# SwiGLU pairs in one decoder block on one core: the product b22 is also made in matmuls of 512 columns, in the first product's two banks

## The chip, the cores and the metric

The kernel is one program on one NeuronCore of a Trainium2 chip. The metric is its time on the device in microseconds (us); the median over runs is compared. A core has a matrix engine (TensorE, PE in the profile; PEld is its loading of stationary weights), a vector engine (VectorE, DVE), an activation engine (ScalarE, ACT), GpSimd (POOL) and SyncE (SP), which here issues the loads. They run side by side and wait for each other through semaphores. Matmuls write into banks of PSUM, which hold 128 partitions x 512 float32 each; everything else is in SBUF or in DRAM.

## The reference, cut to what matters

A decoder block: norm, two token mixers (a convolution and an RG-LRU), a gated merge, a residual, and then a SwiGLU channel mixer with the final norm. The change lies in the channel mixer. With 512 tokens, a model width of 1024 and D_FF = 2816 it computes, in float32:

```
h2  = rmsnorm(x2, norm2_g)                     # 512 x 1024
u   = silu(h2 @ ffn_w1) * (h2 @ ffn_w3)        # 512 x 2816
out = rmsnorm(x2 + u @ ffn_w2, norm_f_g)       # 512 x 1024
```

## The kernel before, in words

The SwiGLU input product is made in 11 "pairs" k = 0 to 10, each of two tiles of 128 columns of D_FF. For a pair the weights form a 2 x 2 block (a half of the 1024 channels by one of the two column tiles), and so do the activations (a half of the channels by a half of the 512 tokens). A scheme with seven block products instead of eight is used, on sums of weight blocks and sums of activation blocks: b11, b21, b22, t1, t2, t3 and t4. Every product is made for both matrices (w1 in the low 256 columns of a bank, w3 in the high ones). Float32 precision comes from splitting weights and activations in a high and a low part and making three matmuls, high x high, high x low, low x high. With four chunks of channels a product is 2 x 4 x 3 = 24 matmuls of 256 columns; `f_product` (L1191) makes them.

Product t1 of pairs 1 to 10 is made otherwise already (`f_wide`, L1201 and L1202). The high and the low part of its activations lie side by side in one tile of 512 columns (`s1b`), so high x high and high x low are one matmul of 512 columns; low x high is one of 256. The two matrices then need a bank each, `fe0` and `fe1`, and each bank holds two halves that have to be added. These two banks come from a PSUM pool of only two buffers (`psum2`), so t1 of the next pair can begin only when both banks have been read. ACT copies the low half into a tile `se` in SBUF (L1298), DVE adds the high half to it (L970), for each bank.

The order of products in the code, and on PE, is for each pair: b11 (for four pairs only; for the others it was made earlier, as was b21), t1, b21, t2, t4 of the pair before, b22, t3. Their sums go like this before the change. t2 is added to b11 in bank `fa`. ACT copies this common sum to a second bank `ft` (L1311). b22 is added to `fa`, t3 to `ft`, and t4 to `ft` as well. After b22, DVE adds `se` to `fa` (L970, 512 columns), ACT makes the silu `sl` (L1264) and DVE the product of the two matrices' halves (L1265). After t3, DVE adds `ft` to `se` and the same two steps follow; after t4 they follow directly from `ft`.

Weights come by SP's loads (`raw_fb`, L352), are summed on DVE (L362 and L119, output `raw_fb`), and split: ACT casts the high part (L123), DVE subtracts it to get the low part (L119). The split tiles are `hl_ft` (for a t product) and `hl_fb` (for a b product), with the pair as suffix in the lists of instructions below. The pool of raw tiles has four buffers, the pool of split tiles five, the pool `short` (`se`, `sl`) five. From pair 7 on, sums of the finished tiles for the output product are made in between on ACT and DVE (`os`, `os1p`, `oe`, `ov`, `ou`). The output product (`or`, L1026) follows the pairs.

Each engine runs its instructions in one fixed order. A scheduler sets it when the program is built, from the code's order and an estimate of times; inside a `manual_schedule` block the named engines keep the code's order.

Of the kernel before, what the change touches and what calls it, by code (L numbers as in the profile page):

```python
# [9 lines left out]
F32R = mybir.dt.float32r  # L10
# [76 lines left out]
def tile_block(ctx, tc, a, out):  # L87
# [9 lines left out]
    def tiles(tag, bufs):  # L97
        p_ = pool(tag, bufs)
        return lambda name, dtype=F32: p_.tile([P, T], dtype, tag=tag, name=name)

    longt, shortt, gatet = tiles("long", SLOTS), tiles("short", SHORT), tiles("gate", GATES)
# [5 lines left out]
    def bank(name):  # L107
        return psum.tile([P, T], F32, tag="mm", name=name)

    def bank2(name):  # L110
        return psum2.tile([P, T], F32, tag="cv", name=name)

    vec, act, pe, pool_e = nc.vector, nc.scalar, nc.tensor, nc.gpsimd
# [77 lines left out]
    def weights(key, ahead=AHEAD):  # L191
        i = next(i for i, c in enumerate(chunks) if c[0] == key)
        emit_to(i + 1 + ahead)
        return held.pop(key)
# [206 lines left out]
    F_ORDER = []  # L401
# [239 lines left out]
    HALVES = [slice(0, 256), slice(256, 512)]  # L641
# [42 lines left out]
    ET = mybir.EngineType  # L684
    with tc.manual_schedule(engines={ET.PE, ET.Activation, ET.DVE, ET.SP}):
# [33 lines left out]
        _, ws, ps = early[0]  # L719
# [235 lines left out]
    for j in range(8):  # L955
        ws = w_tiles(f"lo{j}_0", 5) + w_tiles(f"lo{j}_1", 5)
        ps = bank(f"yb{j}")
# [12 lines left out]
    add = lambda o, x, y: vec.tensor_tensor(out=o, in0=x, in1=y, op=ALU.add)  # L970
    LO, HI = HALVES
# [119 lines left out]
    for n, j in enumerate(mixq.order()):  # L1091
        ws = w_tiles(f"co{j}", ND)
        ps = bank(f"ya{j}")
        mm3(ps, ws, un)
        o = sga[j]
# [11 lines left out]
    for c in range(ND):  # L1107
        if c < ND // 2:
            both_ = longt(f"h2{c}", F32R)
# [70 lines left out]
    o7 = Sevenfold(outq)  # L1180
    f_held = {}

    def f_product(ps, k, x_, w_, again=False, ahead=AHEAD, matrices=range(2)):

        if 0 in matrices:
            f_held[w_, k] = weights(f"f{w_}_{k}", ahead)
        h, l = f_held[w_, k]
        for i in matrices:
            for c, (xh, xl) in enumerate(x_):
                for m, (lw, rx_) in enumerate(((h, xh), (h, xl), (l, xh))):  # L1190
                    pe.matmul(  # L1191
                        ps[:, HALVES[i]], lw[:, 4 * i + c, :], rx_, start=not (again or i or c or m),
                        stop=bool(i and c == 3 and m == 2), skip_group_check=True,
                    )

    def f_wide(banks, k, x_, both_, w_):

        h, l = weights(f"f{w_}_{k}")
        for i, ps in enumerate(banks):
            for c, (xh, _) in enumerate(x_):  # L1200
                pe.matmul(ps, h[:, 4 * i + c, :], both_[c], start=c == 0, stop=False, skip_group_check=True)  # L1201
                pe.matmul(ps[:, LO], l[:, 4 * i + c, :], xh, start=False, stop=c == 3, skip_group_check=True)  # L1202

    kept, opened = {}, {}
# [19 lines left out]
    f_in = {n: [] for n in ("a22", "s1", "s2", "s3", "s4")}  # L1224
# [37 lines left out]
    def f_out(c, dst, sign=1.0):  # L1262
        s_ = shortt("sl")
        act.activation(s_[:, LO], c[:, LO], AF.Silu, scale=sign)  # L1264
        vec.scalar_tensor_tensor(out=dst, in0=c[:, HI], scalar=sign, in1=s_[:, LO], op0=ALU.mult, op1=ALU.mult)  # L1265
# [12 lines left out]
        for k in STARTED[1]:  # L1278
            go_on(k)

    s1_both = [longt(f"s1b{c}", F32R) for c in range(4)]
    for both_, parts_ in zip(s1_both, f_in["s1"]):
        for cs, v in zip(HALVES, parts_):
            nc.sync.dma_start(both_[:, cs].bitcast(F32), v.bitcast(F32))

    seven = {}

    def ffn_product(n, k):

        b_ = seven.setdefault(k, {})  # L1290
        x_ = {"b11": "a11", "b21": "a12", "b22": "s4", "t1": "s1", "t2": "s2", "t3": "s3", "t4": "a22"}[n]
        r = {"b11": "a", "b21": "b", "b22": "a", "t1": "e", "t2": "a", "t3": "c", "t4": "c"}[n]
        if n == "t1" and k:
            wide = [bank2(f"fe{i}_{k}") for i in range(2)]
            f_wide(wide, k, f_in[x_], s1_both, n)
            b_["se"] = shortt(f"se_{k}")
            for cs, ps in zip(HALVES, wide):
                act.copy(b_["se"][:, cs], ps[:, LO])  # L1298
                add(b_["se"][:, cs], ps[:, HI], b_["se"][:, cs])
            return  # L1300
        if n in ("b11", "t1"):
            b_[r] = (bank2 if r == "e" else bank)(f"f{r}_{k}")
        if n == "t2" and k in BEGUN:
            b_[r] = bank(f"f{r}_{k}")
            with tc.issue_after(newest["kept"]):
                act.copy(b_[r], kept[k])
        ps = b_[r]
        f_product(ps, k, f_in[x_], n, n not in ("b11", "t1"))
        if n in ("b11", "t2"):
            new = b_["b" if n == "b11" else "c"] = bank(f"f{n}_{k}")  # L1310
            act.copy(new, ps)  # L1311
            if n == "b11":
                o7.uv[k] = [longt(f"ou{k}"), None]
        elif n == "t1":
            b_["se"] = shortt(f"se_{k}")
            act.copy(b_["se"], ps)
        elif n == "b22":
            add(ps, ps, b_["se"])
        elif n == "t3":
            newest["added"] = add(b_["se"], ps, b_["se"]).ins  # L1320
        if n not in ("b11", "t1", "t2"):
            i, cs = {"b21": (0, LO), "b22": (0, HI), "t3": (1, HI), "t4": (1, LO)}[n]
            if o7.uv[k][i] is None:
                o7.uv[k][i] = longt(f"ov{k}")
            f_out(b_["se"] if n == "t3" else ps, o7.uv[k][i][:, cs], -1.0 if n in ("b22", "t3") else 1.0)
        if n == "t4" and k >= SUMS_FROM:
            o7.pair(k - SUMS_FROM)

    opened_last = list(STARTED[1])
    for n, k in F_ORDER:  # L1330
        ffn_product(n, k)
        if opened_last:
            k = opened_last.pop(0)
            f_out(opened[k], o7.uv[k][0][:, LO])

    x2 = [[longt(f"x2b{t}{h}") for h in range(2)] for t in range(NT)]
    gf = pairt("gf", F32)
# [99 lines left out]
```

## Time and profile before

| | |
|---|---|
| runs before, median (lowest to highest) | 792.45 us (792.34 to 792.89) |
| the profiled execution's own time | 792.59 us |
| its span | 790.8 us |
| the SwiGLU pairs in the trace | 499.0 to 681.2 us |
| busy over the span | PE 99%, DVE 88%, ACT 61%, POOL 28% |

The page of the profile gives busy times, groups of instructions and a chain of work that ended last: the last instruction, what released it, what released that, and so on back to the start. A row of a timeline gives the start and the duration of one instruction (or of several alike in a row, x2), its engine, its line, and output<-inputs by the names above; in square brackets is how long the engine was idle before it and what ended that.

### The profile page before, as it was taken

What the parts mean: (1) busy time and instruction counts of PE and PEld (TensorE: products, weight loads), DVE (VectorE), ACT (ScalarE), POOL (GpSimd) and SP (SyncE); (2) the same over time, 40 slices, a digit from 0 to 9 for tenths busy, and PEclk for the clock granted to TensorE, in tenths of its full rate; (3) what the DMA queues carried; (4) which work ended last, traced back from release to release, by engine and by line L of the source; (5) the groups of instructions that cost most, each with busy time, mean ns of one, the idle gap of its engine ahead of it and who ended that gap; (6) DMA issues with size and microseconds to landing.
All of it is one profiled execution on the core that took longest, in us unless ns stands there. A gap on an engine that the chain in (4) does not pass through costs nothing.

```text
span 790.8 us, 12171 instructions
## 1 busy us (share of the span) xinstructions
PE 783.7 (99%) x4332; PEld 685.9 (87%) x4332; DVE 697.8 (88%) x1050; ACT 483.0 (61%) x712; POOL 222.1 (28%) x172
## 2 busy tenths in 40 slices
PE   9999999999999999999999999999999999999997
PEld 8888888888888888888888899999999999888886
DVE  7699899999989988795797889899989899989867
ACT  7655685987768855562335597555545555585544
POOL 1855766797666856130000000000000000000000
PEclk9999999999999999999999999999999999999999
DMA  6945646487564664458857555554534353786552
GB/s 210 263 130 155 194 137 201 122 244 215 169 201 143 211 186 123 130 173 259 282 185 250 176 168 156 158 154 130 144 107 129 107 149 96 229 291 206 181 173 107
DMA packets 190428, 139.24 MB, mean 176 GB/s; under 512 B 14452, under 2 KB 169504, under 8 KB 190368
## 3 DMA queue, kind: packets, MB, share of 16 engines
q1 hardware_dynamic: 190367, 138.47, 58.0%
q8 instruction: 34, 0.56, 0.3%
q14 instruction: 27, 0.21, 0.1%
HBM read 116.94 MB, written 18.64 MB: 171 GB/s over the span
## 4 chain that ended last, share of the span: by engine, by line
PE 97%; DVE 1%; DMA 1%; issue 0%; SPq 0%; ACT 0%; ACTq 0%
PE z L537 36%; PE or L1026 12%; PE fa L1191 9%; PE ft L1191 8%; PE yb L537 7%; PE ya L537 6%; PE fr L1191 5%; PE mxr L1026 5%; PE g L891 3%; PE fe L1201 2%; PE fb L1191 1%; PE fe L1202 1%; DMA raw_in<-in_w_in_dram 1%; PE th L569 0%; PE z L722 0%; PE fe L1191 0%
## 5 line engine op out<-in xcount | busy, mean ns | idle before, releaser
L766 DVE SCALAR_TENSOR_TENSOR cv<-u,par,cv 128x511 f32<-128x511 f32 (+19 forms) x240 | 162.6, 733 | 5.5 <-ACT cv L763 5.3
L119 POOL TENSOR_TENSOR hl_in<-raw_in,hl_in 128x1024 fp32r<-128x1024 f32 x50 | 121.1, 2427 | 73.5 <-ACT hl_in L123 69.8
L119 POOL TENSOR_TENSOR ows<-ows 128x256 f32<-128x256 f32 x66 | 58.5, 888 | 35.9 <-DMA ows<-in_ffn_w_dram 32.9
L123 ACT CAST hl_ft<-raw_fb 128x1024 fp32r<-128x1024 f32 x44 | 46.0, 1050 | 31.8 <-DVE raw_fb L362 13.3
L119 DVE TENSOR_TENSOR hl_ft<-raw_fb,hl_ft 128x1024 fp32r<-128x1024 f32 x44 | 53.6, 1221 | 9.3 <-ACT hl_ft L123 9.3
L123 ACT CAST hl_in<-raw_in 128x1024 fp32r<-128x1024 f32 x50 | 52.0, 1043 | 12.0 <-PE z L537 6.6
L119 DVE TENSOR_TENSOR hl_fb<-raw_fb,hl_fb 128x1024 fp32r<-128x1024 f32 x33 | 40.0, 1222 | 5.6 <-ACT hl_fb L123 5.5
L362 DVE TENSOR_TENSOR raw_fb<-raw_fb,raw_fb 128x1024 f32<-128x1024 f32 x33 | 40.3, 1221 | 1.5 <-DMA raw_fb<-in_ffn_w_dram 1.2
L123 ACT CAST hl_fb<-raw_fb 128x1024 fp32r<-128x1024 f32 x33 | 34.4, 1051 | 11.5 <-issue 5.0
L537 PE MATMUL z<-h10h,hl_in 128*128 128x512 f32 (+1 forms) x106 | 41.0, 387 | 0.2 <-DVE h10l L593 0.2
L537 PE MATMUL z<-h12h,hl_in 128*128 128x512 f32 (+1 forms) x106 | 40.6, 383 | 0.0
L537 PE MATMUL z<-h13h,hl_in 128*128 128x512 f32 (+1 forms) x106 | 40.6, 383 | 0.0
L537 PE MATMUL z<-h17h,hl_in 128*128 128x512 f32 (+1 forms) x106 | 40.6, 383 | 0.0
L537 PE MATMUL z<-h16h,hl_in 128*128 128x512 f32 (+1 forms) x106 | 40.6, 383 | 0.0
L537 PE MATMUL z<-h11h,hl_in 128*128 128x512 f32 (+1 forms) x106 | 40.5, 383 | 0.0
L537 PE MATMUL z<-h14h,hl_in 128*128 128x512 f32 (+1 forms) x106 | 40.5, 383 | 0.0
L537 PE MATMUL z<-h15h,hl_in 128*128 128x512 f32 (+1 forms) x106 | 40.5, 383 | 0.0
L123 ACT CAST hl_ob<-raw_ob 128x1024 fp32r<-128x1024 f32 (+1 forms) x23 | 23.4, 1015 | 18.6 <-PE or L1026 10.9
L1191 PE MATMUL fa<-hs_1h,hl_fb 128*128 128x256 f32 x176 | 33.5, 283 | 0.0
L1191 PE MATMUL ft<-hs_1h,hl_ft 128*128 128x256 f32 x176 | 33.5, 283 | 0.0
L1191 PE MATMUL fa<-hs_0h,hl_ft 128*128 128x256 f32 x176 | 33.4, 283 | 0.0
L119 DVE TENSOR_TENSOR hl_ob<-raw_ob,hl_ob 128x1024 fp32r<-128x1024 f32 (+1 forms) x23 | 27.1, 1177 | 4.5 <-ACT hl_ob L123 4.2
(958 smaller groups left out, 2519.5 us busy)
## 6 DMA issues: line engine op xcount, KB each, us to landing
raw_fb<-in_ffn_w_dram SPq DMA_DIRECT2D x116, 256.0 KB
raw_in<-in_w_in_dram SPq DMA_DIRECT2D x52, 512.0 KB
ows<-in_ffn_w_dram SPq DMA_DIRECT2D x44, 256.0 KB
os<-ows SPq DMA_DIRECT2D x22, 512.0 KB
raw_ob<-in_ffn_w_dram SPq DMA_DIRECT2D x33, 256.0 KB
raw_ot<-os SPq DMA_DIRECT2D x33, 256.0 KB
raw_lo<-in_lru_w_out_dram SPq DMA_DIRECT2D x16, 320.0 KB
mxws<-in_w_mix_out_dram SPq DMA_DIRECT2D x8, 512.0 KB
```

What stands on the lines that cost most here:

```text
L119: return eng.tensor_tensor(out=o, in0=x, in1=y, op=ALU.subtract)
L123: copy(h, full)
L362: vec.tensor_tensor(out=q, in0=q, in1=y, op=ALU.add)
L537: pe.matmul(ps, l, r, start=i == 0, stop=i == n - 1)
L766: vec.scalar_tensor_tensor(out=acc[c][:, s:], in0=u[c][:, : T - s], scalar=dw(c, s), in1=acc[c][:, s:], op0=ALU.mult, op1=ALU.add)
L891: pe.matmul(ps, l, r, start=k == 0, stop=k == len(mms) - 1)
L1026: pe.matmul(banks[i], l_[:, ts], r_, start=start and n == 0, stop=stop and n == 2, skip_group_check=again)
L1191: pe.matmul(ps[:, HALVES[i]], lw[:, 4 * i + c, :], rx_, start=not (again or i or c or m), stop=bool(i and c == 3 and m == 2), skip_group_c ...
L1201: pe.matmul(ps, h[:, 4 * i + c, :], both_[c], start=c == 0, stop=False, skip_group_check=True)
L1202: pe.matmul(ps[:, LO], l[:, 4 * i + c, :], xh, start=False, stop=c == 3, skip_group_check=True)
```

## The change

For pairs 1 to 10, b22 is made by `f_wide` too, from four more side-by-side tiles (`s4b`, filled by eight more transfers of 128 KB, each half of a tile of 512 columns, behind t1 of pair 0). It accumulates on top of t1 in the banks `fe0` and `fe1`. A new tile `sb` in SBUF receives the two halves of each bank by a copy on ACT (L1296) and an addition on DVE, as `se` does. The common sum after t2 goes to a tile `us` in SBUF (`short`) by the copy that went to the bank `ft` before; `sb` gets `us` added on DVE, and the silu and the product of b22 read `sb`. t3 and t4 accumulate on `fa` itself. The loop over the products stands in a block that keeps PE's order as written.

```diff
-    def f_wide(banks, k, x_, both_, w_):
+    def f_wide(banks, k, x_, both_, w_, again=False):
...
-                pe.matmul(ps, h[:, 4 * i + c, :], both_[c], start=c == 0, stop=False, skip_group_check=True)
+                pe.matmul(ps, h[:, 4 * i + c, :], both_[c], start=c == 0 and not again, stop=False, skip_group_check=True)
                 pe.matmul(ps[:, LO], l[:, 4 * i + c, :], xh, start=False, stop=c == 3, skip_group_check=True)
...
+    def one_tile(name, k, wide):
+
+        o = shortt(f"{name}_{k}")
+        for cs, ps in zip(HALVES, wide):
+            act.copy(o[:, cs], ps[:, LO])
+            add(o[:, cs], ps[:, HI], o[:, cs])
+        return o
...
+        if n == "b22" and k:
+            f_wide(b_["e"], k, f_in[x_], s4_both, n, True)
+            sb = one_tile("sb", k, b_["e"])
+            add(sb, b_["us"], sb)
+            f_out(sb, o7.uv[k][0][:, HI], -1.0)
+            return
         if n == "t1" and k:
-            wide = [bank2(f"fe{i}_{k}") for i in range(2)]
+            wide = b_["e"] = [bank2(f"fe{i}_{k}") for i in range(2)]
             f_wide(wide, k, f_in[x_], s1_both, n)
...
+            b_["se"] = one_tile("se", k, wide)
             return
...
-        if n in ("b11", "t2"):
+        if n == "t2" and k:
+            b_["us"] = shortt(f"us_{k}")
+            act.copy(b_["us"], ps)
+            b_["c"] = ps
+        elif n in ("b11", "t2"):
...
-    for n, k in F_ORDER:
-        ffn_product(n, k)
+    with tc.manual_schedule(engines={ET.PE}):
+        for n, k in F_ORDER:
+            ffn_product(n, k)
+            if (n, k) == ("t1", 0):
+                for both_, parts_ in zip(s4_both, f_in["s4"]):
+                    side_by_side(both_, parts_)
```

The order of products on PE stays, but the order on ACT and DVE shifts. ACT at the end of pair 8, from the cast of t2's weights of pair 9 on, before (`hl_X<-raw_X` are casts of weights, `os1p` is a cast for the output product):

```order
L123 CAST hl_ft_9_6504<-raw_fb_9_6463 128x1024
L1264 ACTIVATE sl<-ft_7_6268 128x256
L123 CAST hl_ft_8_6547<-raw_fb_8_6306 128x1024
L123 CAST os1p_6540<-os_6538 128x256
L123 CAST hl_fb_9_6578<-raw_fb_9_6466 128x1024
L1264 ACTIVATE sl<-fa_6373 128x256
```

and after:

```order
L123 CAST hl_ft_9_6497<-raw_fb_9_6456 128x1024
L1264 ACTIVATE sl<-fa_6229 128x256
L123 CAST hl_ft_8_6540<-raw_fb_8_6302 128x1024
L1296 COPY sb_6559<-fe_8_6397 128x256
L1296 COPY sb_6559<-fe_8_6398 128x256
L123 CAST os1p_6533<-os_6531 128x256
L123 CAST hl_fb_9_6568<-raw_fb_9_6459 128x1024
```

The two copies of `sb`, which wait for the end of b22 of pair 8, now stand ahead of the two casts. DVE at the same place, before:

```order
L119 TENSOR_TENSOR hl_ft_8_6547<-raw_fb_8_6306,hl_ft_8_6547 128x1024
L119 TENSOR_TENSOR os1p_6540<-os_6538,os1p_6540 128x256
L119 TENSOR_TENSOR ov_5061<-ov_5061,oe_6543 128x256
L970 TENSOR_TENSOR fa_6373<-fa_6373,se_6425 128x512
L119 TENSOR_TENSOR oe_6543<-ou_4334,ov_5061 128x256
L119 TENSOR_TENSOR hl_fb_9_6578<-raw_fb_9_6466,hl_fb_9_6578 128x1024
L1265 SCALAR_TENSOR_TENSOR ou_6403<-fa_6373,sl 128x256
```

and after:

```order
L119 TENSOR_TENSOR hl_ft_8_6540<-raw_fb_8_6302,hl_ft_8_6540 128x1024
L119 TENSOR_TENSOR os1p_6533<-os_6531,os1p_6533 128x256
L119 TENSOR_TENSOR ov_5075<-ov_5075,oe_6536 128x256
L970 TENSOR_TENSOR sb_6559<-fe_8_6397,sb_6559 128x256
L119 TENSOR_TENSOR oe_6536<-ou_4334,ov_5075 128x256
L970 TENSOR_TENSOR sb_6559<-fe_8_6398,sb_6559 128x256
L119 TENSOR_TENSOR hl_fb_9_6568<-raw_fb_9_6459,hl_fb_9_6568 128x1024
L970 TENSOR_TENSOR sb_6559<-us_6495,sb_6559 128x512
```

The two additions that free the banks stand where the addition of `se` to `fa` stood, and the third comes behind the next split. DVE at the end of pair 9, before:

```order
L119 TENSOR_TENSOR hl_ft_9_6726<-raw_fb_9_6469,hl_ft_9_6726 128x1024
L119 TENSOR_TENSOR oe_6722<-ou_4995,ov_5255 128x256
L970 TENSOR_TENSOR fa_6637<-fa_6637,se_6632 128x512
L119 TENSOR_TENSOR hl_fb_10_6757<-raw_fb_10_6645,hl_fb_10_6757 128x1024
L1265 SCALAR_TENSOR_TENSOR ou_4704<-fa_6637,sl 128x256
```

and after:

```order
L119 TENSOR_TENSOR hl_ft_9_6716<-raw_fb_9_6462,hl_ft_9_6716 128x1024
L119 TENSOR_TENSOR oe_6712<-ou_5009,ov_5266 128x256
L970 TENSOR_TENSOR sb_6735<-fe_9_6601,sb_6735 128x256
L970 TENSOR_TENSOR sb_6735<-fe_9_6602,sb_6735 128x256
L119 TENSOR_TENSOR hl_fb_10_6744<-raw_fb_10_6635,hl_fb_10_6744 128x1024
L970 TENSOR_TENSOR sb_6735<-us_6671,sb_6735 128x512
```

Here too the additions that free the banks have taken the place of the addition on `fa`; everything ahead of them kept its order.

More of the change, by code (lines that the diff above doesn't have):

```diff
@@ L1279, in tile_block, with side_by_side @@
             go_on(k)
-    s1_both = [longt(f"s1b{c}", F32R) for c in range(4)]
-    for both_, parts_ in zip(s1_both, f_in["s1"]):
+    s1_both, s4_both = ([longt(f"{n}b{c}", F32R) for c in range(4)] for n in ("s1", "s4"))
+    def side_by_side(both_, parts_):
         for cs, v in zip(HALVES, parts_):
             nc.sync.dma_start(both_[:, cs].bitcast(F32), v.bitcast(F32))
+    for both_, parts_ in zip(s1_both, f_in["s1"]):
+        side_by_side(both_, parts_)
     seven = {}
+    def one_tile(name, k, wide):
[4 more added lines that the diff above has]
+        return o
     def ffn_product(n, k):
@@ L1292, in ffn_product @@
         r = {"b11": "a", "b21": "b", "b22": "a", "t1": "e", "t2": "a", "t3": "c", "t4": "c"}[n]
+        if n == "b22" and k:
[4 more added lines that the diff above has]
+            return
         if n == "t1" and k:
-            wide = [bank2(f"fe{i}_{k}") for i in range(2)]
+            wide = b_["e"] = [bank2(f"fe{i}_{k}") for i in range(2)]
             f_wide(wide, k, f_in[x_], s1_both, n)
[L1296 to L1299, printed above, removed]
+            b_["se"] = one_tile("se", k, wide)
             return
@@ L1329, in tile_block @@
     opened_last = list(STARTED[1])
-    for n, k in F_ORDER:
-        ffn_product(n, k)
-        if opened_last:
-            k = opened_last.pop(0)
-            f_out(opened[k], o7.uv[k][0][:, LO])
+    with tc.manual_schedule(engines={ET.PE}):
[3 more added lines that the diff above has]
+                for both_, parts_ in zip(s4_both, f_in["s4"]):
+                    side_by_side(both_, parts_)
+            if opened_last:
+                k = opened_last.pop(0)
+                f_out(opened[k], o7.uv[k][0][:, LO])
     x2 = [[longt(f"x2b{t}{h}") for h in range(2)] for t in range(NT)]
```

## Prediction

> **What bounds the kernel now.** I read the page's busy times and its chain first, then busy times over the stretch of the SwiGLU pairs, then the chain in order of time there, and last the timelines of DVE, ACT and SP where DVE runs late.
>
> ```profile
> PE 783.7 (99%) x4332; PEld 685.9 (87%) x4332; DVE 697.8 (88%) x1050; ACT 483.0 (61%) x712; POOL 222.1 (28%) x172
> ...
> PE 97%; DVE 1%; DMA 1%; issue 0%; SPq 0%; ACT 0%; ACTq 0%
> ```
>
> PE is busy for 99% of the span and makes 97% of the chain, so a gain must come from PE's own work, and any wait put on PE costs its full length.
>
> ```profile
> 499.00:681.20 182.20, 182.20 (x1440) 178.04 (x1439) 165.21 (x211) 98.64 (x152) 0.00 (x0) 1.00 0.45 132
> 639.00:681.20 42.20, 42.20 (x333) 41.04 (x333) 40.02 (x59) 23.96 (x39) 0.00 (x0) 1.00 0.44 136
> ```
>
> The columns are the stretch, its length, busy us of PE, weight loads, DVE, ACT and POOL, the granted clock, and the transfers. Over all pairs PE never idles. DVE is idle for 182.20 - 165.21 = 17.0 us, but only for 2.2 us of the last 42: there it is nearly as full as PE.
>
> ```profile
> 565.34 0.23 PE fe L1201
> ...
> 614.14 0.23 PE fe L1201
> ...
> 642.83 2.88 PE fa L1191 x24
> 645.71 2.88 PE ft L1191 x24
> 648.59 0.23 PE fe L1201
> ...
> 651.42 2.87 PE fa L1191 x24
> ...
> 660.06 2.88 PE ft L1191 x24
> 662.94 0.23 PE fe L1201
> ...
> 677.28 0.93 PE or L1026 x4
> 678.22 3.03 PE ft L1191 x24
> 681.24 97.29 PE or L1026 x428
> ```
>
> The chain shows start and length. A narrow product takes 2.88 us (b22 of pair 8 from 642.83, t3 from 645.71). A wide one, t1 of pair 9, takes 651.42 - 648.59 = 2.83. The other rows give where t1 of pairs 4, 7 and 10 start: 565.34, 614.14, 662.94.
>
> **The change part by part.**
>
> *PE.* Ten products go from 2.88 to 2.83 us: 0.05 each, **-0.5** in all. All of it is on the path, if nothing else makes PE wait. It is also the largest gain that these rows allow.
>
> *DVE and ACT, work.* Durations come from the starts of neighbours on DVE, where it runs without a pause:
>
> ```profile
> 645.60 0.42 DVE L119 TENSOR_TENSOR os1p<-os,os1p 128x256 fp32r<-128x256 f32 x1
> 645.93 0.42 DVE L119 TENSOR_TENSOR ov<-ov,oe 128x256 f32<-128x256 f32 x1
> 646.26 0.69 DVE L970 TENSOR_TENSOR fa<-fa,se 128x512 f32<-128x512 f32 x1
> 646.86 0.42 DVE L119 TENSOR_TENSOR oe<-ou,ov 128x256 f32<-128x256 f32 x1
> 647.20 1.22 DVE L119 TENSOR_TENSOR hl_fb<-raw_fb,hl_fb 128x1024 fp32r<-128x1024 f32 x1
> ...
> 651.86 0.76 DVE L970 TENSOR_TENSOR se<-fe,se 128x256 f32<-128x256 f32 x2
> 653.86 1.23 DVE L362 TENSOR_TENSOR raw_fb<-raw_fb,raw_fb 128x1024 f32<-128x1024 f32 x1 [1.24 <-DMA raw_fb<-in_ffn_w_dram]
> ...
> 670.74 0.69 DVE L119 TENSOR_TENSOR ous2l<-ou,ous2h 128x512 fp32r<-128x512 f32 x1
> ...
> 651.46 0.37 ACT L1298 COPY se<-fe 128x256 f32<-128x256 f32 x1 [0.20 <-PE fe L1202]
> ```
>
> 256 columns occupy DVE for 0.33 us (645.60 to 645.93), 512 for 0.60 (646.26 to 646.86), and 512 from SBUF alone take the same 0.69 as from PSUM (670.74 against 646.26). Before, b22 needs one addition of 512. After, it needs two of 256 and one of 512: +0.66 us per pair, 6.6 in ten. It lies beside PE's work as long as DVE's 17.0 us of idle time cover it; in the last 42 us they are 2.2, so there it can show. ACT gets two more copies of 0.37 (the row at 651.46) per pair, 7.4 us into 182.20 - 98.64 = 83.6 of idle time: free as work, not free in order (below). The copy of the common sum stays, of the same size, to another place. That t3 and t4 now accumulate on `fa` adds no wait: t4 of the pair before and b22, 5.7 us, lie between t2's end and t3.
>
> *Eight more transfers on SP.* Their kind is in the trace, for `s1b`:
>
> ```profile
> 493.19 0.51 SPq L1284 DMA_DIRECT2D s1b<-hs_0l  x1
> 493.80 0.55 SPq L1284 DMA_DIRECT2D s1b<-hs_0h  x1
> ...
> 506.67 1.23 DVE L119 TENSOR_TENSOR hl_ft<-raw_fb,hl_ft 128x1024 fp32r<-128x1024 f32 x1 [1.29 <-ACT hl_ft L123]
> ...
> L1201 PE MATMUL fe<-s1b,hl_ft x80: 395/398/403, 513.5 to 665.2; 128*128 128x512 f32 x80
> ```
>
> They are issued 0.61 us apart, so eight hold SP's queue for 4.9 us at most, ahead of loads of weights. The nearest consumer is t1 of pair 1: its weights are split by 506.67 + 1.23 = 507.90 and PE needs them at 513.5. The 5.6 us between cover 4.9; my estimate is some 2 us of delay, from where the transfers stand among the loads. The first b22 made wide is later still. Cost 0; without the cover it would be at most the 4.9.
>
> *The release of the two banks.* This is the new wait. Before, t1 of the next pair finds both banks read long ago. After, they are held until b22's `sb` additions. In DVE's order these stand where the addition on `fa` stands in the rows here, so that row says when they come:
>
> ```profile
> 562.66 0.69 DVE L970 TENSOR_TENSOR fa<-fa,se 128x512 f32<-128x512 f32 x1
> ...
> 611.47 0.69 DVE L970 TENSOR_TENSOR fa<-fa,se 128x512 f32<-128x512 f32 x1
> ...
> 662.21 1.23 DVE L119 TENSOR_TENSOR hl_ft<-raw_fb,hl_ft 128x1024 fp32r<-128x1024 f32 x1
> 663.34 0.42 DVE L119 TENSOR_TENSOR oe<-ou,ov 128x256 f32<-128x256 f32 x1
> 663.68 0.70 DVE L970 TENSOR_TENSOR fa<-fa,se 128x512 f32<-128x512 f32 x1
> ...
> 677.35 0.69 DVE L970 TENSOR_TENSOR se<-ft,se 128x512 f32<-128x512 f32 x1
> ```
>
> For pair 3 the addition starts at 562.66 and t1 of pair 4 at 565.34: a first addition of 0.42 leaves 2.3 us. For pair 6 it is 611.47 against 614.14, also 2.2; for pair 8, 646.26 against 648.59, 1.9. What DVE and ACT do later than before comes off these margins: I expect 1.0 to 1.1 us to be left at pairs 3, 6 and 8, so **0** there. The second bank is used half a product, 1.42 us, later and has more. For pair 9 the addition starts at 663.68, *after* t1 of pair 10 at 662.94. DVE was 3.6 us behind b22's end at 660.06 without anyone waiting; now PE waits.
>
> How much later DVE stands at 663.68 than before is set one pair earlier:
>
> ```profile
> 644.58 0.41 ACT L123 CAST os1p<-os 128x256 fp32r<-128x256 f32 x1 [0.39 <-DVE os L970]
> 645.79 1.05 ACT L123 CAST hl_fb<-raw_fb 128x1024 fp32r<-128x1024 f32 x1 [0.81 <-PE fa L1191]
> ...
> 648.45 1.83 SPq L352 DMA_DIRECT2D raw_fb<-in_ffn_w_dram  x3
> ```
>
> The `os1p` cast at 644.58 now stands behind two copies that wait for b22 of pair 8, which ends at 645.71 less the 0.4 that eight wide b22 have gained: 645.31. The second copy occupies ACT till about 645.7, the cast till 646.03, and DVE's `os1p` starts at 646.06 instead of 645.60. Then come `ov` 646.40, the first `sb` addition 646.73, `oe` 647.06, the second 647.40, and `hl_fb` 647.73 instead of 647.20: 0.53 later. SP's load at 648.45 is issued when that split has ended (647.20 + 1.22 = 648.42), so it lands 0.53 later and DVE, which waited 1.24 us for it, resumes at 654.39 instead of 653.86. Its own work is done at 652.62 (651.86 + 0.76) + 0.53 + 0.60 = 653.75, so this wait takes up all lateness but the 0.53. From there DVE runs without a pause to 663.68, in the same order in both kernels. The first `sb` addition of pair 9 then starts at 663.68 + 0.53 = 664.21 and ends at 664.63; t1 of pair 10 starts some 0.06 later, at 664.69. PE would be ready at 662.94 - 9 x 0.05 = 662.49: a wait of 2.2 us. Against before, t1 starts 664.69 - 662.94 = +1.75 later; b22 of pair 10 still gives back 0.05: **+1.7**.
>
> Bounds for this step: if DVE is not late at all, 663.68 + 0.42 + 0.06 - 662.94 = +1.2. If none of the 0.66 of nine pairs (5.9) is absorbed, 1.2 + 5.9 = +7.1. I take +1.7, near the lower end, because the DVE wait at 653.86 absorbs. As the forecast's own spread I take +1.2 to +2.3 (a second 0.53 from a pair's ACT order).
>
> *Behind it.* t4 of pair 10 writes the bank that DVE's addition at 677.35 has read by 678.04; it starts at 678.22, behind four `or` matmuls. DVE there is 0.53 + 2 x 0.66 = 1.85 later at most, about 1.65 with a pause taken up, and PE is 1.7 later, with one more `or` matmul of 0.93 / 4 = 0.23 ahead: no further wait. The 97.29 us of `or` shift as a whole.
>
> **The sum** on the profiled execution of 792.59 (0.14 above the median): -0.45 + 2.2 - 0.05 = +1.7, 794.3. On the median, 792.45 + 1.7 = **794.2**. A measurement here can tell about 0.2%, 1.6 us, from no change: below 790.9 is faster, above 794.0 slower.
>
> **The rivals.**
>
> *PE does not wait (not slower).* The mechanism is the same bank at pair 9; it decides if the first `sb` addition ends before 662.5, 1.6 us sooner than the row at 663.68 ends its first 0.42. For it: DVE idles 1.24 us at 653.86, so a load landing sooner would move all behind it. Against: that load hangs on the split before, which comes later. Then only -0.5 stays: 791.95. The same time results if the additions are issued sooner than I read.
>
> *More banks come late.* DVE does not recover its 0.66 per pair, and t1 of pairs 4, 5, 7 or 9 waits as well. It decides when DVE is some 1.0 us later than I assume at pairs 3, 6 or 8. For it: the margins of 1.0 are small beside six pairs' 4.0 us of work, and copies at the head of ACT's order delay casts. Against: 17.0 us of idle time. Between the +2.3 and +7.1 I take half of the 5.9 absorbed: 1.2 + 2.95 = 4.15, 796.6.
>
> *The wait lowers PE's clock.* PE hardly ever pauses in this trace; the nearest row is at the start:
>
> ```profile
> 8.00:9.60 1.60, 1.24 (x10) 0.96 (x9) 1.41 (x5) 1.42 (x4) 0.41 (x1) 1.00 1.14 326
> ```
>
> There PE was idle for 0.36 of 1.60 us, and the granted clock stayed 1.00; no row shows a pause of 2.2 us. If one product behind the wait were made at half the pace, it would cost another 2.88: 797.1. The Trainium skill, TensorE: Matmul & The Clock Gate, section "What's actually happening", says that the array's clock is halved after an idle window of about 3.4 us and restored after a busy one of that length; by it a wait of 2.2 us would change nothing if it stays shorter than the window, which speaks for my sum, and a longer one (the second rival) would bring this case about. No run here shows it.
>
> *Matmuls of 512 columns are cheaper in a long stream (faster).* If high x (high, low) cost as much as one narrow matmul, 2.88 / 24 = 0.12, a b22 would fall to 16 x 0.12 = 1.92, and ten give -9.6: 782.9. Against: ten such products already stand in this trace, at 2.83. The same page, section "Back-to-back issue gap", gives about 131 ns for 512 columns in a sustained stream; by that figure, as an estimate, a b22 would take 8 x (0.131 + 0.12) = 2.0 us. The trace disagrees (8 x (x + 0.12) = 2.83 makes x 0.23), and the measurement decides.
>
> **How the numbers follow.** Forecast .52: its spread of +1.2 to +2.3 ends at 793.65 to 794.75, so .24 of it lies within 0.2% and .28 above. No wait .14 (same). More banks late .27 (slower). Clock .03 (slower). Cheaper matmuls .04 (faster). That is faster .04, same .38, slower .58. The range 791.9 to 796.6 leaves out the cheaper matmuls, the clock and nearly half of the second rival (.12): .19. The forecast's own range is 793.6 to 794.8.
>
> **What would show it.** In the profile after: b22 on `fe` at 2.83 us; t1 of pair 10 starting 2 us behind t3's end with DVE's `sb` addition as the releaser; no such wait at t1 of pairs 4, 7 and 9; an ACT `os1p` cast behind the `sb` copies and a `hl_fb` split half a us later at pair 8. If PE waits at other pairs too, or not at pair 10, or the wait is not DVE's, the prediction is wrong.

## The result and the profile after

The changed kernel takes 797.17 us in the median of its first six runs (795.83 to 798.38), against 792.51 before: a ratio of 1.0058 with a 95% interval of 1.0045 to 1.0070. It is slower by 4.7 us, not by 1.7, and its runs lie far apart, where those of before stay within 0.6 us. The profiled execution took 797.93 us with a span of 796.2. Two executions of this case, one of the kernel before (1308.6 us, granted clock 0.556) and one of e7 below (4348.6 us, 0.168), are in the slow state and stay out of the ratios.

Busy times and chain of the changed kernel:

```profile
PE 784.9 (99%) x4252; PEld 683.0 (86%) x4252; DVE 701.8 (88%) x1070; ACT 488.3 (61%) x732; POOL 220.7 (28%) x172
...
PE 91%; DVE 5%; DMA 2%; issue 1%; ACT 1%; SPq 0%; ACTq 0%; DVEq 0%
```

The shares of busy time are those of before. The chain is not: DVE and DMA now hold 7% of it, where PE alone held 97%. The table of waits on PE in the stretch of the pairs (us in total, times, the longest) says for what:

```profile
PE fe L1201 <- DVE sb L970: 4.1, 2, 2.5
```

The busy times by stage (stretch, length, PE, weight loads, DVE, ACT, POOL, granted clock, transfers) say where:

```profile
520.00:540.00 20.00, 17.46 (x118) 16.27 (x118) 18.14 (x27) 10.09 (x19) 0.00 (x0) 0.91 0.59 170
...
660.00:690.00 30.00, 28.46 (x197) 26.42 (x197) 28.45 (x46) 17.81 (x32) 0.00 (x0) 1.00 0.40 130
```

PE waits twice, both times for a bank that a `sb` addition still reads: once between 660 and 690, and once, longer, between 520 and 540. There the granted clock is 0.91 as well. PE's timeline at both places:

```profile
530.58 0.28 PE L1191 MATMUL fa<-hs_1h,hl_ft 128*128 128x256 f32 x1
533.39 0.50 PE L1201 MATMUL fe<-s1b,hl_ft 128*128 128x512 f32 x1 [2.54 <-DVE sb L970]
...
533.85 0.40 PE L1201 MATMUL fe<-s1b,hl_ft 128*128 128x512 f32 x1
...
535.07 0.63 PE L1201 MATMUL fe<-s1b,hl_ft 128*128 128x512 f32 x1
...
537.63 0.41 PE L1191 MATMUL fa<-hs_0h,hl_ft 128*128 128x256 f32 x1
...
668.32 0.47 PE L1201 MATMUL fe<-s1b,hl_ft 128*128 128x512 f32 x1 [1.53 <-DVE sb L970]
```

The first wait, 2.54 us, is at t1 of pair 2. A microsecond behind it the 512-column matmuls go from 0.40 to 0.63 us, and the product takes 537.63 - 533.39 = 4.24 us instead of 2.83. The second wait, 1.53 us, is the forecast one at t1 of pair 10. Waits of 2.54 and 1.53, some 1.5 for the slower clock, less 0.5 of gain: 5.1 of the 5.3 us by which this execution (797.93) lies above that of before (792.59).

Why DVE is late at pair 2 starts 25 us earlier. The kernel before, from the timelines of SP's queue (from 490 to 505) and of DVE, and the start of t1 of pair 2 from its chain:

```profile
496.37 7.40 SPq L352 DMA_DIRECT2D raw_fb<-in_ffn_w_dram  x8
...
504.16 1.23 DVE L362 TENSOR_TENSOR raw_fb<-raw_fb,raw_fb 128x1024 f32<-128x1024 f32 x1
...
528.85 0.69 DVE L970 TENSOR_TENSOR fa<-fa,se 128x512 f32<-128x512 f32 x1
...
530.88 0.23 PE fe L1201
```

And SP's queue, in the same stretch, and DVE in the changed kernel:

```profile
500.97 0.60 SPq L1285 DMA_DIRECT2D s4b<-hs_1l  x1
501.67 3.35 SPq L352 DMA_DIRECT2D raw_fb<-in_ffn_w_dram  x6
...
508.52 1.23 DVE L362 TENSOR_TENSOR raw_fb<-raw_fb,raw_fb 128x1024 f32<-128x1024 f32 x1 [4.33 <-DMA raw_fb<-in_ffn_w_dram]
...
532.93 0.74 DVE L970 TENSOR_TENSOR sb<-fe,sb 128x256 f32<-128x256 f32 x2
```

The loads of pair 1 began at 496.37; behind the eight `s4b` transfers they begin at 501.67, 5.3 us later. DVE's sum for t1 of pair 1 moves from 504.16 (the `raw_fb` sum of before) to 508.52. From there DVE catches up hardly anything until the `sb` additions of pair 1, at 532.93, where the addition on `fa` stood at 528.85. t1 of pair 2 waits for the first of them.

### The profile page after: what moved, and what is told of

It is laid out like the page before. It is cut to its first block, busy times and chain, and to the rows that moved or that the text cites. A ratio compares the mean times of both kernels' runs of the same rounds, so it can differ in the third digit from the quotient of the medians.

```text
span 796.2 us, 12060 instructions
## 1 busy us (share of the span) xinstructions
PE 784.9 (99%) x4252; PEld 683.0 (86%) x4252; DVE 701.8 (88%) x1070; ACT 488.3 (61%) x732; POOL 220.7 (28%) x172
## 4 chain that ended last, share of the span: by engine, by line
PE 91%; DVE 5%; DMA 2%; issue 1%; ACT 1%; SPq 0%; ACTq 0%; DVEq 0%
PE z L537 35%; PE or L1026 12%; PE fa L1191 10%; PE yb L537 7%; PE ya L537 5%; PE fr L1191 5%; PE mxr L1026 5%; PE fe L1201 4%; PE g L891 3%; PE fe L1202 2%; DVE hl_ft L119 1%; PE fb L1191 1%; DVE raw_fb L362 1%; DMA raw_in<-in_w_in_dram 1%; DMA raw_fb<-in_ffn_w_dram 1%
## 5 line engine op out<-in xcount | busy, mean ns | idle before, releaser
L1201 PE MATMUL fe<-s1b,hl_ft 128*128 128x512 f32 x80 | 30.1, 414 | 4.1 <-DVE sb L970 4.1
L1191 PE MATMUL fa<-hs_1h,hl_ft 128*128 128x256 f32 x160 | 30.4, 283 | 0.0
```

The lines of the kernel that those rows point to most:

```text
L1191: pe.matmul(ps[:, HALVES[i]], lw[:, 4 * i + c, :], rx_, start=not (again or i or c or m), stop=bool(i and c == 3 and m == 2), skip_group_c ...
L1201: pe.matmul(ps, h[:, 4 * i + c, :], both_[c], start=c == 0 and not again, stop=False, skip_group_check=True)
```

## The experiments

All changes are against the changed kernel unless said otherwise. The times of before beside them were taken on the same chip.

**The changed kernel again (e1_again).**

> The changed kernel once more, for its spread. Its six runs lie in two groups, 795.8 to 796.4 and 797.9 to 798.4 us. Theory clock: the groups differ by whether TensorE's granted clock falls behind the wait at t1 of pair 2; the runs near 798 have a mean clock of 0.996 to 0.997 and those near 796 of 0.998 to 1.0, and nothing lies between. Rival: the wait itself varies, then the times spread without groups and do not go with the clock.

Six runs: 793.88 to 797.74, median 796.91 against 792.59 (ratio 1.0050, 1.0036 to 1.0063). The times do not form two groups with nothing between: 793.88 lies below them, and 795.69, 796.49 and 797.34 close most of the gap. The clock, though, divides the twelve runs of this kernel as the first theory says: the six from 797.34 us up have a mean granted clock of 0.996 or 0.997, the six up to 796.49 one of 0.998 or more. The profile is of the 793.88 run; from its timelines of DVE and PE:

```profile
505.64 1.23 DVE L362 TENSOR_TENSOR raw_fb<-raw_fb,raw_fb 128x1024 f32<-128x1024 f32 x1 [1.94 <-DMA raw_fb<-in_ffn_w_dram]
...
530.35 0.75 DVE L970 TENSOR_TENSOR sb<-fe,sb 128x256 f32<-128x256 f32 x2
...
530.82 0.50 PE L1201 MATMUL fe<-s1b,hl_ft 128*128 128x512 f32 x1 [0.46 <-DVE sb L970]
...
664.25 0.47 PE L1201 MATMUL fe<-s1b,hl_ft 128*128 128x512 f32 x1 [1.54 <-DVE sb L970]
```

And its busy times at pair 2, in the columns of above:

```profile
520.00:540.00 20.00, 19.54 (x146) 18.55 (x146) 18.49 (x25) 10.18 (x16) 0.00 (x0) 1.00 0.58 167
```

Here the same loads let DVE go on at 505.64, not 508.52; the wait at pair 2 is 0.46 us, the clock stays at 1.00, and the wait at pair 10 is again 1.54. So the lateness behind the transfers itself varies between executions, by 2.9 us in these two. Of these, 1.2 are there already when SP issues the loads (at 500.43 in e1_again, 501.67 in the first profile); why the rest of the time to landing differs is open. Together with the clocks, the times fit a short wait, a long wait, and a long wait with a slower clock; only two of the twelve executions have a profile.

**The transfers behind the loads of pair 1 (e2_late).**

```diff
-            if (n, k) == ("t1", 0):
+            if (n, k) == ("b22", 0):
                 for both_, parts_ in zip(s4_both, f_in["s4"]):
```

> The eight s4b transfers are issued behind the weight loads of pair 1 instead of ahead of them; nothing else changes. Theory transfers (the loads of pair 1 land 4.3 us later, DVE is as late until pair 1's sb additions, so t1 of pair 2 waits 2.5 us): that wait is gone and only the one at t1 of pair 10 is left, as the prediction had it: 794.2 us, and no fall of the clock at pair 2. Rival work (DVE's 0.66 us more per pair makes the lateness): t1 of pair 2 still waits over 1 us, 796 to 798.

792.85 us in eleven runs (792.53 to 792.97) against 792.59: ratio 1.0003 (0.9994 to 1.0012). The wait at pair 2 and the spread are gone, as the theory of the transfers says: moving the eight transfers takes 4.1 us off the 796.91 of e1_again, some of it at pair 10 (below). The other wait is shorter than it had it:

```profile
504.42 1.23 DVE L362 TENSOR_TENSOR raw_fb<-raw_fb,raw_fb 128x1024 f32<-128x1024 f32 x1 [0.20 <-DMA raw_fb<-in_ffn_w_dram]
...
528.91 0.75 DVE L970 TENSOR_TENSOR sb<-fe,sb 128x256 f32<-128x256 f32 x2
...
663.29 0.47 PE L1201 MATMUL fe<-s1b,hl_ft 128*128 128x512 f32 x1 [0.78 <-DVE sb L970]
```

DVE is on time, and t1 of pair 10 waits 0.78 us. One move of a few transfers made the scheduler order ACT differently too: at pair 8 the `os1p` cast now stands between the two `sb` copies and no longer behind both. ACT in e2_late:

```profile
644.02 0.38 ACT L1296 COPY sb<-fe 128x256 f32<-128x256 f32 x1
644.29 0.41 ACT L123 CAST os1p<-os 128x256 fp32r<-128x256 f32 x1
645.39 0.37 ACT L1296 COPY sb<-fe 128x256 f32<-128x256 f32 x1 [0.69 <-PE fe L1202]
```

ACT in e1_again:

```profile
644.21 0.37 ACT L1296 COPY sb<-fe 128x256 f32<-128x256 f32 x1
645.58 0.37 ACT L1296 COPY sb<-fe 128x256 f32<-128x256 f32 x1 [0.99 <-PE fe L1202]
645.85 0.41 ACT L123 CAST os1p<-os 128x256 fp32r<-128x256 f32 x1
```

The cast comes 1.5 us sooner. This is the head of ACT's order that the prediction priced, undone by accident; the 0.76 us between the two waits goes with it, but other orders moved as well, so that is not shown alone.

**Banks of even pairs from the other pool (e3_banks).**

```diff
-            wide = b_["e"] = [bank2(f"fe{i}_{k}") for i in range(2)]
+            wide = b_["e"] = [(bank2 if k % 2 else bank)(f"fe{i}_{k}") for i in range(2)]
```

> The wide banks of even pairs come from the other PSUM pool (six banks), so t1 of the next pair never needs a bank that sb still holds; the transfers stay where the change put them. Theory banks: both waits (pair 2 and pair 10) vanish though DVE is as late as in the changed kernel, 792.0 us (the gain of 0.45 alone). Rival: DVE's lateness makes PE wait for weights instead, 794 or more.

794.36 us (793.76 to 795.49) against 792.59: 1.0023 (1.0015 to 1.0032). Both waits for `sb` are gone with the transfers in place, and in this profile DVE is late at pair 2 (it goes on at 506.34 and reaches the `sb` additions of pair 1 at 532.19). So the held banks are what turns DVE's lateness into PE's there. But not to 792.0: other waits stand in the profile. From the table of waits, and below it from PE's timeline:

```profile
PEld fa L1191 <- ACT fa L1321: 1.0, 2, 0.6
```

```profile
697.50 1.43 PE L1026 MATMUL or<-hl_ob,ous4h 128*128 128x512 f32 x5 [0.30 <-ACT ous4h L123]
```

t2 waits for ACT's copy of the kept sum, and the output product for the sums `ous4` that ACT and DVE make for it. Each theory had half of it.

**Before, with the transfers alone (e4_copies).** The eight transfers are put into the kernel before at the same place; nothing reads them.

> The kernel before with only the eight s4b transfers added at the place that the change gives them; nothing reads them. Theory: loads and DVE are 4 us late around 508 to 530 but no bank is held for DVE, so PE does not wait, 792.5 us (within 0.3). Rival: the transfers cost time by themselves, 794 or more.

792.79 us against 792.59: 1.0004 (0.9995 to 1.0013). DVE is late here too, and PE does not wait:

```profile
506.46 1.23 DVE L362 TENSOR_TENSOR raw_fb<-raw_fb,raw_fb 128x1024 f32<-128x1024 f32 x1 [2.28 <-DMA raw_fb<-in_ffn_w_dram]
...
532.03 0.69 DVE L970 TENSOR_TENSOR fa<-fa,se 128x512 f32<-128x512 f32 x1
```

The addition on `fa` comes 3.2 us later than before (528.85) and costs nothing. (One of the eleven runs, at 794.30, has no profile.) It needs both parts of the change, late loads and held banks, to make the wait.

**PE kept busy in the wait (e5_fill, e12_fill_half).** Twenty matmuls of 256 columns, or five of 512, into a spare bank ahead of t1 of pair 2:

```diff
+            if k == 2:
+                spare = bank("spare")
+                h_, _ = f_held["t3", 1]
+                for i in range(FILL):
+                    pe.matmul(spare[:, LO], h_[:, i % 8, :], f_in["s1"][i % 4][0], start=True, stop=True, skip_group_check=True)
             f_wide(wide, k, f_in[x_], s1_both, n)
```

> The changed kernel with 20 more matmuls of 256 columns into an unread bank of PSUM ahead of t1 of pair 2; their results are not used. They take 20 x 0.12 = 2.4 us, about the longest wait seen there. Theory clock (a wait of 2.5 us lets the clock fall, and the half clock then costs 1.6 us): t1 of pair 2 starts no later than it did after the long wait, the clock stays at 1.00, and every run comes out at -0.5 + 2.4 + 1.5 = +3.4, near 796.0 us, none above 796.6. Rival: the clock falls for another reason, then runs of 797 to 798.4 remain.

(As run, e5 does not compute the block: its twenty matmuls each start an accumulation anew in one half of their bank, and they disturb a sum of the block; which one was not looked into. The other instructions and their sizes are those of the changed kernel. In e12 the five open and close one whole bank, and it does compute the block.) 795.41 us, 794.81 to 795.83 in five runs, against 792.76: 1.0033 (1.0020 to 1.0046). Though 2.4 us of useless matmuls were added, it is 1.5 us faster than the median of e1_again, and no run is above 795.83. Half of that is another thing: the scheduler gave e5 the order of e2 on ACT, and its wait at pair 10 is 0.78 us instead of 1.54.

```profile
530.73 2.56 PE L1318 MATMUL spare<-hs_0h,hl_ft 128*128 128x256 f32 x20
533.18 0.50 PE L1202 MATMUL fe<-s1b,hl_ft 128*128 128x512 f32 x1
```

DVE is as late here as in the changed kernel's first profile (the `sb` additions start at 532.71, there at 532.93), so without the twenty PE would have paused about as long. t1 of pair 2 starts at 533.18, near the 533.39 there, without a pause. The busy times from 533.3 to 537.9 in the changed kernel:

```profile
533.30:537.90 4.60, 4.51 (x18) 3.89 (x19) 4.60 (x8) 0.85 (x2) 0.00 (x0) 0.65 0.73 207
```

And in e5_fill:

```profile
533.30:537.90 4.60, 4.60 (x31) 4.24 (x32) 4.60 (x7) 1.91 (x4) 0.00 (x0) 1.00 0.77 226
```

The granted clock is 0.65 behind the pause and 1.00 without it, so it falls because of the pause. The sum comes out as well: -0.5 + 2.4 + 0.8 = 2.7, measured 2.65.

> As e5, with 5 matmuls of 512 columns into the spare bank (5 x 0.23 = 1.2 us, not used), so that a part of the wait at t1 of pair 2 stays. Theory clock (only the long pause of some 2.5 us lets the clock fall): the pause that is left is at most 1.4 us and the clock stays at 1.00, so the runs lie between -0.5 + 1.2 + 0.8 = +1.5 (794.1 us, DVE little late) and -0.5 + 2.5 + 0.8 = +2.8 (795.4, DVE as late as in the first profile), none above 796. Rival (any pause may lower the clock): some runs of 796.5 to 798.

794.96 us against 792.84 (1.0032, 1.0021 to 1.0042). Seven of eight runs lie between 794.5 and 795.54, as expected; one, at 796.56, does not, and it has no profile, so whether its clock fell or its loads came later still stays open (its mean granted clock is 0.998). In none of the thirteen runs of e5 and e12 is that mean below 0.998, where six of the twelve of the changed kernel had 0.996 or 0.997.

```profile
530.78 1.33 PE L1318 MATMUL spare<-s1b,hl_ft 128*128 128x512 f32 x5
533.18 0.51 PE L1202 MATMUL fe<-s1b,hl_ft 128*128 128x512 f32 x1 [1.07 <-DVE sb L971]
```

In the profiled run a pause of 1.07 us was left, and the clock of this stretch stayed at 1.00.

Two profiles of experiments further down (e9, e10) hold long pauses at another place, t4 of pair 10, from other waits. PE of e9 and the busy times behind it, then the same of e10:

```profile
683.20 0.58 PE L1191 MATMUL fa<-h24h,hl_ft 128*128 128x256 f32 x1 [2.52 <-DVE se L970]
683.20:687.80 4.60, 4.60 (x25) 4.58 (x26) 2.69 (x5) 0.94 (x3) 0.00 (x0) 0.65 0.40 139
```

```profile
683.64 0.39 PE L1191 MATMUL fa<-h24h,hl_ft 128*128 128x256 f32 x1 [2.25 <-DVE se L970]
683.60:688.20 4.60, 4.56 (x25) 4.56 (x26) 2.73 (x5) 0.93 (x2) 0.00 (x0) 0.63 0.39 134
```

The clock falls there as well. So in the profiles of this case all three pauses of 2.25 us and more in the pairs were followed by a lower clock, and none of those up to 1.54 us was.

**The transfers on another queue (e8_queue).** `side_by_side` issues `s4b` by `nc.gpsimd.dma_start`, at the same place in the program.

> The changed kernel with the eight s4b transfers issued by GpSimd's queue, at the same place in the program, so they stand ahead of no weight load. Theory order (SP issues one after the other, the loads of pair 1 wait behind them): DVE is on time at pair 1 and only t1 of pair 10 waits, 1.5 us: 793.6 us. Rival bandwidth (the transfers take the loads' share wherever they are issued): DVE is still over 2 us late at pair 1, 795 or more.

792.90 us against 792.76: 1.0000 (0.9991 to 1.0008). From DVE's timeline, and below it a row of the list of what uses `s4b` (GpSimd's issues, with the first and the last start):

```profile
504.20 1.23 DVE L362 TENSOR_TENSOR raw_fb<-raw_fb,raw_fb 128x1024 f32<-128x1024 f32 x1 [0.17 <-DMA raw_fb<-in_ffn_w_dram]
```

```profile
L1285 POOL DMA_DIRECT2D s4b<-hs_1h x4: 538/538/686, 475.5 to 487.8; - x4
```

DVE is on time, so off SP's queue the transfers cost nothing. But the second row (four of the eight; the others are issued from 476.8 to 491.1) shows that the same bytes did not move at the same time: GpSimd issued them all before SP's loads, which start at 496.19, while SP in the changed kernel issued them from 496.50 to 500.97. So e8 does not decide between the two theories. That the place in SP's queue costs time is seen in the 5.3 us by which the loads are issued later; whether the transfers' share of bandwidth adds to it was not separated. (The wait at pair 10 is 0.8 us here, again with e2's order on ACT.)

**Without the last wait (e6_late9, e7_both).** e6 is e2 with b22 of pair 9 in narrow matmuls on `fa`, the copy of t2's sum to a bank included:

```diff
+NARROW = (0, 9)
...
-        if n == "b22" and k:
+        if n == "b22" and k not in NARROW:
...
-        if n == "t2" and k:
+        if n == "t2" and k not in NARROW:
```

> As e2 (transfers behind the loads of pair 1), and b22 of pair 9 is made as before the change, in narrow matmuls on fa, so no bank waits for DVE ahead of t1 of pair 10. Theory banks: the last wait (0.8 us in e2) is gone and 9 x 0.05 = 0.45 us of gain is left, 792.1 us. Rival: DVE's work in the last pairs costs time anyway, 792.8.

e7 is e2 and e3 together.

> Transfers as in e2 and banks as in e3. Theory banks: no wait for a bank at all, 792.1 us if the small waits of e3 (on ACT's copy of the kept sum, and 0.9 us in the output product) came from DVE's lateness. Rival: they came from the new order on ACT and DVE, then 793 to 794.

Both lie further above before than e2 did (0.26 us), though the intervals overlap: e6 793.48 us against 792.76 (1.0010, 1.0001 to 1.0019), e7 793.36 (1.0008, 0.9999 to 1.0017). No t1 waits for a bank in either. The wait has moved to the output product. Busy times of e6 there, and below them a row of its PE:

```profile
692.00:700.00 8.00, 7.70 (x34) 6.03 (x33) 5.74 (x10) 4.50 (x7) 0.00 (x0) 1.00 1.04 377
700.00:708.00 8.00, 7.57 (x32) 5.61 (x31) 6.99 (x11) 7.68 (x12) 0.00 (x0) 1.00 0.68 237
```

```profile
705.27 1.91 PE L1027 MATMUL or<-hl_ob,ous6h 128*128 128x512 f32 x7 [0.32 <-ACT ous6h L124]
```

Before, each of these stretches holds 37 matmuls; here 34 and 32, eight fewer at 8.00 / 37 = 0.22 us: 1.7 us. Ahead of `or`, PE had won its 0.5; the sums `ous4` and `ous6` were not ready sooner, and more than the gain is lost on them. The times are those of the rivals; which of their causes it is, DVE's work or the new order, these two runs do not separate.

**The third addition on GpSimd (e9_pool, e10_both_pool).** In e2 and in e7:

```diff
-            add(sb, b_["us"], sb)
+            pool_e.tensor_tensor(out=sb, in0=sb, in1=b_["us"], op=ALU.add)
```

> As e2, and the third addition of each pair (sb plus the common sum, both in SBUF) is made by GpSimd, which is idle in this stretch, instead of DVE; DVE then has 0.06 us more per pair than before the change instead of 0.66. Theory DVE (what is left of the gain is eaten by DVE's work in the last pairs, as a wait at t1 of pair 10 or in the output product): DVE stands some 0.6 us earlier at pair 9, the 0.8 us wait shrinks below 0.3 and the output product does not wait, 792.2 us against e2's 792.85 and 792.6 to 792.8 before. Rival: the slower addition on GpSimd delays the silu and the product behind it on DVE, 793 or more.

> As e7 (late transfers, banks from two pools), and the third addition of each pair on GpSimd. Theory DVE: with no bank to wait for and DVE's load as before, neither the pairs nor the output product wait: -0.45, 792.2 us, against e7's 793.36. Rival: the waits in the output product come from the order of the sums for it, not from DVE's load: 793 or more.

799.0 us and 798.85 against 792.64 (1.0076, 1.0063 to 1.0088; 1.0073, 1.0061 to 1.0086). The group on GpSimd in e9, and below it the table of DVE's waits:

```profile
L1308 POOL TENSOR_TENSOR sb<-sb,us 128x512 f32<-128x512 f32 x10 | 19.3, 1932 | 309.5 <-DVE sb L970 309.5
```

```profile
DVE ou L1265 <- ACT sl L1264: 11.1, 9, 1.6
```

One addition takes 1.93 us there instead of 0.69. The silu starts that much later, DVE stands behind it for up to 1.6 us in its fixed order, and with it everything that PE needs: 6.0 us saved as work, 11.1 lost as waits. PE then pauses for DVE and its clock falls (the rows of e9 and e10 above). The test says nothing on DVE's load alone.

**Wide b22 in pairs 1 to 6 only (e11_late6).** As e6, with `NARROW = (0, 7, 8, 9, 10)`.

> As e2, with b22 wide only in pairs 1 to 6; pairs 7 to 10, where DVE also makes sums for the output product, are as before the change. Theory DVE: six pairs have idle time for 0.66 us each, so 6 x 0.05 = 0.3 us is won and nothing waits: 792.3 to 792.5 us. Rival: the lateness of six pairs (4 us of work) is carried into the last ones and the output product waits, 793 or more.

792.21 us (eleven runs, 792.0 to 792.99) against 792.64: 0.9997 (0.9988 to 1.0006). PE is busy throughout from 520 to 760; its rows from 660 on:

```profile
660.00:690.00 30.00, 30.00 (x203) 27.63 (x202) 28.11 (x47) 16.74 (x26) 0.00 (x0) 1.00 0.56 176
690.00:760.00 70.00, 70.00 (x311) 57.95 (x310) 61.01 (x88) 43.86 (x62) 0.00 (x0) 1.00 0.69 223
```

This is the lowest median of all: it is 0.43 us below that of before, where 0.3 was expected, but the interval does not separate it from no change. The six early pairs do absorb their 0.66 us of DVE work.

## Why the prediction was wrong, point by point

**The step that failed: "Eight more transfers on SP", put at a cost of 0.** Its upper bound, 4.9 us of delay in SP's queue, was about right (5.3 in the first profile, 4.1 in e1_again); the "some 2 us" that it took instead was not. And it looked at one consumer, the weights of t1 of pair 1, which were indeed ready in time. It did not follow DVE further: DVE runs almost without a pause from there to 529, so 4.1 us of lateness came out at the `sb` additions of pair 1, and a term put at 0 cost a wait of 2.54 us and, behind it, 1.5 us of slower clock in that execution. The step on the banks listed margins for pairs 3, 6, 8 and 9 and left out pair 1, whose 528.85 (plus 0.42) against t1 of pair 2 at 530.88 left 1.6 us; 4.1 less 1.6 is the wait of 2.5. e2 and e8 (wide b22, transfers out of the loads' way) and e4 (transfers alone) cannot be told from before, and e3 (both, but no bank held) has no wait there: it takes late loads and held banks together.

**The wait at t1 of pair 10: right place, mis-sized.** 2.2 us was forecast, 1.54 measured in both profiles of the changed kernel. The 0.53 us of lateness carried from pair 8 was not there. In e1_again the split `hl_fb` ended 0.8 us later than before, as the order on ACT had it, but the load behind it did not land later:

```profile
653.91 1.22 DVE L362 TENSOR_TENSOR raw_fb<-raw_fb,raw_fb 128x1024 f32<-128x1024 f32 x1
...
663.68 0.75 DVE L970 TENSOR_TENSOR sb<-fe,sb 128x256 f32<-128x256 f32 x2
```

DVE went on at 653.91 without a wait for the transfer, and the first `sb` addition stands at 663.68, exactly where the addition on `fa` stood. So the lower bound, +1.2 for a DVE that is not late, was the value to take; the execution with hardly any wait at pair 2 came out there, 793.88 against 792.59. Two readings behind the 0.53 do not hold. From 653.86 on DVE does pause, for 0.51 us at 656.20 in before (for a cast on ACT that follows DVE's own sum, so it absorbs nothing), and its order is not quite the same: the product `ov` that stood at 661.21 is made at 657.46 in e1_again. And the 0.06 us from the addition's end to t1, which no row showed, were 0.15 (663.68 + 0.42 to 664.25).

**The clock: a rival given .03, and true in several runs.** Its price of one product at half pace, 2.88 us, was too high: from the start of t1 of pair 2 to the end of t4 of pair 1 the changed kernel takes 537.84 + 5.91 - 533.39 = 10.36 us by the first row below (from its chain), and e1_again 533.91 + 5.76 - 530.82 = 8.85 by the second (from the chain of that execution): 1.5 us. The slower stretch begins only 1.2 us after PE resumes and lasts some 3.5 us. Its place was wrong as well: pair 2, not pair 10. That the rival's 797.1 lies beside the measured 797.17 is chance, since it adds too high a price to a sum that lacks the wait at pair 2.

```profile
537.84 5.91 PE fa L1191 x48
```

```profile
533.91 5.76 PE fa L1191 x48
```

The Trainium skill, TensorE: Matmul & The Clock Gate, section "What's actually happening", puts the idle window at about 3.4 us; here pauses of 2.54, 2.52 and 2.25 us were enough, while pauses of 0.78 to 1.54 left the clock at 1.00. The measurement decides.

**What held.** b22 on `fe` takes 2.83 us. No t1 of pairs 4, 5, 7 and 9 waits in any profile of the changed kernel, so the margins of 1.0 us and DVE's idle time sufficed, and "more banks come late" did not happen as written, though one more bank did come late, by another cause and at a pair that it does not name. t4 of pair 10 does not wait. With the transfers out of the way (e8, e2) what is left is the forecast mechanism, a smaller wait at pair 10 (0.78 us, with another order on ACT than the one that was forecast from), at +0.1 to +0.3 us.

**What the -0.5 is worth.** The sum took it as won on PE. e6 and e7 show that, with no bank to wait for, the output product waits for its own sums. e11, without the additional work in pairs 7 to 10, has no such wait. That fits a DVE with hardly any idle time in the last pairs (2.2 us before the change), but the orders on ACT and DVE differ between these kernels as well; which of the two it is was not separated, since the attempt to take the work off DVE (e9, e10) brought a longer wait of its own.

## What to carry to other kernels

When a step is moved or added on a queue, follow the lateness that it makes along the next engine until a pause absorbs it, and check every consumer on the way, the buffers it must release too, not only the nearest one. An engine that is late without harm becomes the bound as soon as a change lets another engine wait for it: list every place where the new release is awaited, the first included. And where PE is busy for 99% and its neighbour for 88%, look first where the neighbour has room: here half a microsecond saved on PE was lost again in the last pairs, and whether the early pairs keep their 0.3 us these runs cannot tell from none.

## What the runs showed of the hardware

Pauses of 2.54, 2.52 and 2.25 us on PE were each followed, at once or up to 1.2 us after work resumed, by some 3.5 us at a lower clock (512-column matmuls of 0.63 us instead of 0.40 in the first), which cost about 1.5 us; pauses of 0.78 to 1.54 us were not, and with the pause filled by useless matmuls the clock stayed at 1.00. The same loads, issued behind the same transfers, let DVE go on 2.9 us apart in two executions (505.64 and 508.52), so a kernel whose runs lay within 0.6 us came to spread over 4.5 us. An addition of 128x512 float32 took 1.93 us on GpSimd against 0.69 on DVE.
